# Shorter float16 routing chain, expert indices asked for earlier, and eight expert blocks loaded ahead in a two-block transformer kernel

## The chip, the cores and the metric

The kernel runs on one core of a Trainium2 chip. The metric is the device time of one execution in microseconds (us). Every stage named below runs on the same five engines, each of which works through its own queue of instructions in order: TensorE (PE, matmuls), VectorE (DVE), ScalarE (ACT), GpSimd (POOL) and SyncE (SP, which only issues transfers). A transfer (DMA) is issued from the queue of SP, ACT or POOL, and an instruction that has to wait for a semaphore holds back everything behind it in its queue.

## What is computed

The reference is two transformer blocks of width 1024 on 256 tokens. The change lies in the second half of the first block, a product-key mixture of experts ("peer") with 16384 experts of rank one:

```python
def peer(h, w_pq, sub_keys, u_emb, v_emb):
    q = (h @ w_pq).reshape(B, S, PEER_HEADS, 2, PEER_DHALF)          # 8 heads, two halves of 128
    sc = jnp.einsum("bshcd,hcnd->bshcn", q, sub_keys)                # 128 keys for each half
    s_top, i_top = lax.top_k(sc, PEER_TOPK)                          # best 16 of each half
    cand = s_top[..., 0, :, None] + s_top[..., 1, None, :]
    cand_idx = i_top[..., 0, :, None] * N_KEYS + i_top[..., 1, None, :]
    best, pos = lax.top_k(cand.reshape(B, S, 8, 256), PEER_TOPK)     # best 16 of 256 sums
    expert_idx = jnp.take_along_axis(cand_idx, pos, axis=-1)
    gate = jax.nn.softmax(best, axis=-1)
    ...
    a = gelu(einsum("ced,cd->ce", u_emb[idx], hx)); out = einsum("ce,ced->cd", g * a, v_emb[idx])
```

So every token gets 8 x 16 experts with a gate each. Before it stand the convolution and attention of the first block, behind it the second block; neither is edited.

## The kernel before

**Query stage** (about 276 to 336 us of the profiled execution). The weights of the queries come in 16 chunks of 128x1024, weight numbers 66 to 81. A chunk is loaded by SP, copied rounded by ACT into `whi` (L143), and the remainder `wlo` is `raw - whi`, computed by POOL for the numbers in the table `POOL` and by DVE otherwise (L145, L147). PE then runs 24 matmuls for the chunk (L166 to L168 in turn: each group of three needs `whi` twice and `wlo` once, so a chunk can't get far without its `wlo`), ACT evicts the query as `pq` (L948), and PE and ACT make the scores `sc` (L933, L935) two chunks later.

**Routing chain** on DVE. `unit(tt, h, ..)` finds the top 16 of the two score rows of head h for the token half tt: per row two MAX8, two FIND_INDEX8 and a MATCH_REPLACE8 (`top16`, L850 to L858), then a CAST of the 16 indices into `tops` (L873), then sums of candidates `cd` (L880) and their own top 16 (`best`, `pos`). There are 16 units, 8 for each half. Units, selects and gates stand in a background list `self.bg`, from which `pump` issues a budget of work per chunk (QP) or expert block (UP). `select(tt, h0)` turns four heads' positions into key numbers by a one-hot compare (`eq`, L911), a product with `tops` (L915, by DVE for half 1 and by POOL for half 0) and a sum (L917). `gates(tt)` makes the expert number `ei` and the gate `ex`, and asks for later steps by `later(n, ..)`, n expert blocks behind: `ask` (the pick of indices for the gathered rows, two matmuls of `ei` with `spread` per L1622), `exp`, `softmax` and `turn` (the transposes L986 on PE, and the pick of the gates).

**Which tokens go which way.** Tokens 0 to 159 (N = 160) run dense over all 128 blocks of 128 experts. The other 96 tokens are served by gathered rows: `RowGroup` (`ROWS`: 64 tokens from 192, 32 tokens from 160) fetches, by POOL's indirect DMA (L1632), 128 single expert rows at a time into one of RB = 8 `row` buffers, and DVE takes the dot product (L1637) and later the weighted sum (L1647). `some_rows(RU)` asks for RU of such transfers per u block and `some_rows(RV)` for RV per v block.

**The u stage** (336 to 669 us): per expert block i one load of 512 KB from a ring of ten buffers that are called raw, whi and wlo in turn, 8 matmuls `mm<-hn,raw` (L1031; 16 records in the trace, since each float32 matmul leaves two), and a Gelu on ACT. From the end of `self.bg` on (block `i0`), the one-hot stage runs beside the remaining blocks: 40 groups of four tokens, each with DVE's one-hots `QO` (L1055), ACT's `P`, POOL's `R`, eight matmuls (`place`, L1069) and a multiplication into the matrix G (`put`, L1079).

**The v stage** (674 to 970 us): 4 matmuls with a zero operand open the accumulators (L1146; `zeros` is set by DVE just ahead, L1144), then 123 of the 128 v blocks run with 8 matmuls each (L1141). Every fourth load of v blocks is issued from POOL's queue, the others from SP's, and the gathers run beside it. Between the first 64 blocks and the others `park` (the residual stream) is loaded back as `xo` by POOL's queue (L1158), into space that was that of `G1`.

All from the u stage to the end of the v loop is issued in the order of the program text on every engine (`in_order`).

Of the kernel before, what the change touches and what calls it, by code (L numbers as in the profile page):

```python
# [9 lines left out]
F32 = mybir.dt.float32  # L10
F32R = mybir.dt.float32r
# [12 lines left out]
D = 1024  # L24
# [22 lines left out]

N_WT = 279
# [13 lines left out]
POOL = (*range(4, 52), *range(66, 82))  # L62
# [12 lines left out]
UP = (2.1, 1.4)  # L75

RU = 0.8
RV = 0.8

GL = (2, 3, 4)  # L80
# [3 lines left out]


ROWS = ((192, 64), (160, 32))
# [5 lines left out]
class Kernel:  # L92
# [736 lines left out]
    def peer(self):  # L829
# [11 lines left out]
        gTl = p2h.tile([128, T], F16, name="gTl")  # L841
        sk = p2q.tile([128, 16, 128], F32, name="sk")
# [4 lines left out]
        BIG = -3.0e38  # L847

# [13 lines left out]
        tops = p2t.tile([128, 2, 2, 8, 16], F32, name="tops")  # L862

        def unit(tt, h, scs):
# [3 lines left out]
            for c in range(2):  # L868
# [4 lines left out]
                nc.vector.tensor_copy(tops[:, tt, c, h], iu)  # L873
# [12 lines left out]
        def select(tt, h0, eng):  # L886
# [5 lines left out]
            f = p2t.tile([128, 4, m], F32, name="f", bufs=1)  # L892
# [5 lines left out]
            z = p2t.tile([128, m], F32, name="z", bufs=1)  # L898
# [9 lines left out]
            yield 1.2  # L908
            for c, dst in ((0, isel), (1, jsel)):
                eq = p2t.tile([128, m, 16], F32, name="eq", bufs=1)  # L910
                nc.vector.tensor_tensor(eq, f[:, c, :, None].to_broadcast([128, m, 16]),  # L911
                                  self.iota[:, None, :16].to_broadcast([128, m, 16]), op=ALU.is_equal)
                yield 1.1
                e4 = eq.rearrange("p (h s) a -> p h s a", s=16)
                eng.tensor_tensor(e4, e4, tops[:, tt, c, h0:h0 + nh, None, :].to_broadcast([128, nh, 16, 16]), op=ALU.mult)  # L915
                yield 1.1
                nc.vector.reduce_sum(dst[:, tt, h0:h0 + nh].rearrange("p h s -> p (h s)"), eq, axis=AX.X)  # L917
                yield 1.1
# [41 lines left out]
        def gates(tt):  # L960
# [30 lines left out]
            if tt == 1:  # L991
                self.later(GL[0], ask)
# [8 lines left out]
        pr = self.open("rows", side="right")  # L1001
# [25 lines left out]
        def ublock(i, n_t):  # L1027
            raw = whole(a["ut"][i], i)
# [58 lines left out]
        self.bg[k:k] = [select(1, 0, nc.vector), select(1, 4, nc.vector), gates(1)]  # L1087
        self.bg += [select(0, 0, nc.gpsimd), select(0, 4, nc.gpsimd), gates(0)]
# [46 lines left out]
        zero = self.cp.tile([128, 128], F32R, name="zero")  # L1135
        nc.vector.memset(zero.bitcast(F32), 0.0)
# [574 lines left out]
def _constants():  # L1711
# [3 lines left out]
    def put(name, v):  # L1715
        c[:v.shape[0], CST[name]:CST[name] + v.shape[1]] = v
# [134 lines left out]
```

## Time and profile before

| What | us |
|---|---|
| Median of three runs | 1626.1 |
| The three runs | 1626.78, 1626.1, 1613.58 |
| The profiled execution, its own time | 1624.07 |
| Span of that execution in the trace | 1622.2 |
| PE busy | 1533.6 |
| DVE busy | 1167.7 |
| ACT busy | 645.1 |
| POOL busy | 514.1 |

The rows of the trace have a start (us from the start of the span), a duration, the engine, the line of the program and the operands as out<-in; in brackets stands how long the engine stood idle before, and what ended that. Numbers of buffers are left out. A line of a helper collects all its callers, so a stage is best read by a window of time. Durations of neighbouring matmuls overlap: what a run of them costs is the difference of two starts.

### The profile page before, as it was taken

The numbers are of one execution on the slowest core, as the hardware profiler recorded it, in microseconds if no ns is written. First come the engines' busy times: TensorE is split into PE (matmuls) and PEld (weight loads), VectorE is DVE, ScalarE is ACT, GpSimd is POOL, SyncE is SP. The second block draws the span as 40 slices with busy tenths as digits, with TensorE's granted clock in tenths as the row PEclk, the third lists the DMA queues.
The fourth block names the chain that finished last, engine by engine and source line by source line (L and its number), as shares of the span: only waits on it lengthen the run. The fifth ranks groups of instructions, "written<-read, shape, count | busy, mean of one in ns | idle before, by whom it ended". The sixth has DMA issues, their size and how long they took to land.

```text
span 1622.2 us, 29850 instructions
## 1 busy us (share of the span) xinstructions
PE 1533.6 (95%) x11502; PEld 1469.1 (91%) x11502; DVE 1167.7 (72%) x2549; ACT 645.1 (40%) x1387; POOL 514.1 (32%) x379
## 2 busy tenths in 40 slices
PE   8989989996989999999979999999999999999997
PEld 7877989996989999899979999898999998899986
DVE  6998888998888889744434447977777557776755
ACT  4566655531155444100000005366555455654543
POOL 3734632701576777655444520100000020000000
PEclk9999999997999999999989999999999999999999
DMA  5523446475999999999999984743765677366653
GB/s 187 169 91 98 131 139 222 141 248 221 332 349 404 397 393 394 347 409 409 409 374 409 409 344 153 251 126 109 225 185 187 188 191 220 117 195 183 182 185 114
DMA packets 109389, 398.97 MB, mean 246 GB/s; under 512 B 12484, under 2 KB 12643, under 8 KB 108736
## 3 DMA queue, kind: packets, MB, share of 16 engines
q1 hardware_dynamic: 73872, 266.37, 48.3%
q0 software_dynamic: 35232, 130.64, 21.4%
q8 instruction: 90, 1.47, 0.4%
q14 instruction: 51, 0.42, 0.1%
q10 hardware_dynamic: 144, 0.07, 0.0%
HBM read 394.86 MB, written 6.11 MB: 247 GB/s over the span
## 4 chain that ended last, share of the span: by engine, by line
PE 69%; DVE 17%; DMA 7%; issue 3%; ACT 2%; POOL 2%; SPq 0%; POOLq 0%; DVEq 0%; ACTq 0%
PE ax L1141 12%; PE mm L1031 12%; PE mm L166 11%; PE mm L167 11%; PE mm L168 11%; DMA raw<-vv 5%; DVE ax L617 2%; PE mm L234 2%; PE mm L232 2%; PE mm L233 1%; DVE wlo L147 1%; PE ax L1069 1%; DVE junk L1637 1%; DMA raw<-wst 1%; PE ax L471 1%
## 5 line engine op out<-in xcount | busy, mean ns | idle before, releaser
L143 ACT ACTIVATE whi<-raw 128x1024 fp32r<-128x1024 f32 x275 | 290.0, 1058 | 609.3 <-DMA raw<-wst 304.0
L147 DVE TENSOR_TENSOR wlo<-raw,whi 128x1024 fp32r<-128x1024 f32 x211 | 258.0, 1225 | 116.5 <-ACT whi L143 112.5
L166 PE MATMUL mm<-xgh,whi 128*128 128x256 f32 x1064 | 304.1, 286 | 0.0
L167 PE MATMUL mm<-xgl,whi 128*128 128x256 f32 x1064 | 301.1, 283 | 2.6 <-DVE xgl L406 2.6
L168 PE MATMUL mm<-xgh,wlo 128*128 128x256 f32 x1064 | 300.7, 283 | 0.4 <-DVE wlo L147 0.4
L1647 DVE SCALAR_TENSOR_TENSOR acc<-row,w,acc 128x1024 f32<-128x1024 f32 x94 | 120.8, 1285 | 155.1 <-DMA row<-vv,idx 154.8
L167 PEld LDWEIGHTS mm<-xgl,whi 128*128 128x128 f32 x1064 | 201.8, 190 | 3.0 <-DVE xgl L406 2.8
L166 PEld LDWEIGHTS mm<-xgh,whi 128*128 128x128 f32 x1064 | 201.6, 190 | 2.0 <-issue 1.3
L168 PEld LDWEIGHTS mm<-xgh,wlo 128*128 128x128 f32 x1064 | 201.8, 190 | 0.7 <-DVE wlo L147 0.6
L145 POOL TENSOR_TENSOR wlo<-raw,whi 128x1024 fp32r<-128x1024 f32 x64 | 153.8, 2411 | 129.4 <-ACT whi L143 127.7
L1632 POOL DMA_INDIRECT row<-vv,idx x96 | 124.0, 1292 | 89.5 <-DMA row<-vv,idx 61.3
L1632 POOL DMA_INDIRECT row<-un,idx x96 | 110.2, 1147 | 110.4 <-DVE idf L1626 54.3
L1141 PE MATMUL ax<-G,raw 128*128 128x160 f32 x832 | 124.2, 303 | 10.8 <-DMA raw<-vv 10.8
L1141 PEld LDWEIGHTS ax<-G,raw 128*128 128x128 f32 x832 | 117.1, 192 | 12.0 <-DMA raw<-vv 12.0
L1031 PE MATMUL mm<-hn,raw 128*128 128x160 f32 x816 | 121.1, 303 | 1.8 <-issue 1.8
L1637 DVE CUSTOM_DVE_ANT_0 junk<-row,h 128x1024 f32<-128x1024 f32 x96 | 120.5, 1255 | 0.5
L1031 PEld LDWEIGHTS mm<-hn,raw 128*128 128x128 f32 x816 | 114.5, 192 | 2.4 <-issue 2.4
L167 PE MATMUL mm<-hl,whi 128*128 128x256 f32 x368 | 106.6, 290 | 2.2 <-DVE hl L377 2.1
L1141 PE MATMUL ax<-G,wlo 128*128 128x160 f32 x608 | 94.1, 308 | 9.8 <-DMA wlo<-vv 9.6
L1141 PEld LDWEIGHTS ax<-G,wlo 128*128 128x128 f32 x608 | 88.2, 196 | 11.4 <-DMA wlo<-vv 11.3
L617 DVE SCALAR_TENSOR_TENSOR ax<-u,cw,ax 128x256 f32<-128x256 f32 x227 | 97.4, 482 | 0.6
L1031 PE MATMUL mm<-hn,wlo 128*128 128x160 f32 x608 | 93.3, 308 | 0.0
(437 smaller groups left out, 3361.7 us busy)
## 6 DMA issues: line engine op xcount, KB each, us to landing
raw<-wst SPq DMA_DIRECT2D x278, 512.0 KB
raw<-ut SPq DMA_DIRECT2D x51, 512.0 KB
raw<-vv SPq DMA_DIRECT2D x40, 512.0 KB
whi<-ut SPq DMA_DIRECT2D x39, 512.0 KB
wlo<-ut SPq DMA_DIRECT2D x38, 512.0 KB
whi<-vv SPq DMA_DIRECT2D x32, 512.0 KB
wlo<-vv SPq DMA_DIRECT2D x25, 512.0 KB
wlo<-vv POOLq DMA_DIRECT2D x13, 512.0 KB
```

The lines of the kernel that those rows point to most:

```text
L143: nc.scalar.activation(hi, raw, AF.Copy)
L145: nc.gpsimd.tensor_sub(lo, raw, hi)
L147: self.pin = nc.vector.tensor_sub(lo, raw, hi)
L166: nc.tensor.matmul(pt, w[:, s], xs[0][:, k], start=first, stop=False)
L167: nc.tensor.matmul(pt, w[:, s], xs[1][:, k], start=False, stop=False)
L168: nc.tensor.matmul(pt, lo[:, s], xs[0][:, k], start=False, stop=last)
L617: nc.vector.scalar_tensor_tensor(y[:, c] if k == 30 else ps, u[:, c, k:k + T], cw[:, c, k:k + 1], ps, op0=ALU.mult, op1=ALU.add)
L1031: nc.tensor.matmul(pt, raw[:, k * 128:(k + 1) * 128], hn[:, k, :N], start=(k == 0), stop=(k == C - 1))
L1141: nc.tensor.matmul(acc[d // 2][:, d % 2, :N], raw[:, d * 128:(d + 1) * 128], G(i), start=False, stop=False, skip_group_check=True)
L1632: self.k.nc.gpsimd.indirect_dma_start(t, None, table, bass.IndirectOffsetOnAxis(ap=self.idx[:, s:s + 1], axis=0))
L1637: self.k.nc.vector.tensor_tensor_reduce(junk, row, self.h, 1.0, 0.0, ALU.mult, ALU.add, self.a[:, s:s + 1])
L1647: self.k.nc.vector.scalar_tensor_tensor(self.acc, row, w, self.acc, op0=ALU.mult, op1=ALU.add)
```

## The change

1. `tops` becomes float16 and holds each index 16 times over. It is written by POOL (32 CASTs of 128x256, `tops<-iu`) instead of DVE (32 CASTs of 128x16).
2. `select` works in float16: `eq` is laid out so that the last dimension is contiguous in every operand, both halves' products run on DVE, and the sum is four float16 additions (8, 4, 2 and 1 of 16) instead of a reduction.
3. Weight numbers 70 and 76 leave the table `POOL`, so DVE makes their `wlo`.
4. The `rows` pool is opened before the query stage, and its eight buffers receive the first eight u blocks, issued from ACT's queue. The ring starts with block 8, and the v blocks' numbering with 120 instead of 128.
5. The tables `spread`, `fold` and `own` of each row group are loaded from the constants (two transfers on ACT's queue), where six DVE operations had made them.
6. `ask` comes 1 block behind gates(1) (was 2, with `exp`); `exp`, `softmax` and `turn` come 4, 6 and 8 blocks behind (were 2, 3, 4). UP, RU and RV are 1.5/1.3, 0.85 and 0.78 (were 2.1/1.4, 0.8 and 0.8), and some costs of background steps are other numbers.
7. The zero operand of the accumulators' opening is a 128x128 tile that POOL sets early; 16 matmuls of 128 columns replace the 4 of 512. The 512 column `zeros` tile is gone. `pg` and `rows` are closed in the other order, and `xo` then lies elsewhere: the load of `xo` waits for `R` (POOL) and `P` (ACT) of the one-hot stage, and no longer for the last matmul of the first 64 v blocks.

```diff
-POOL = (*range(4, 52), *range(66, 82))
+POOL = (*range(4, 52), *range(66, 70), *range(71, 76), *range(77, 82))
...
-UP = (2.1, 1.4)
-RU = 0.8
-RV = 0.8
-GL = (2, 3, 4)
+UP = (1.5, 1.3)
+RU = 0.85
+RV = 0.78
+AL = 1
+GL = (4, 6, 8)
...
+        zero = self.cp.tile([128, 128], F32R, name="zero")
+        nc.gpsimd.memset(zero.bitcast(F32), 0.0)
...
+        pr = self.open("rows", side="right")
+        first = [pr.tile([128, D], F32, name="row", bufs=RB) for _ in range(RB)]
+        for i, raw in enumerate(first):
+            nc.scalar.dma_start(raw, a["ut"][i])
...
-        tops = p2t.tile([128, 2, 2, 8, 16], F32, name="tops")
+        tops = p2t.tile([128, 2, 2, 8, 16, 16], F16, name="tops")
+        num = p2t.tile([128, 16, 16], F16, name="num")
+        nc.gpsimd.tensor_copy(num, self.iota[:, :16, None].to_broadcast([128, 16, 16]))
...
-                nc.vector.tensor_copy(tops[:, tt, c, h], iu)
+                nc.gpsimd.tensor_copy(tops[:, tt, c, h], iu[:, :, None].to_broadcast([128, 16, 16]))
...
-                eq = p2t.tile([128, m, 16], F32, name="eq", bufs=1)
-                nc.vector.tensor_tensor(eq, f[:, c, :, None].to_broadcast([128, m, 16]),
-                                  self.iota[:, None, :16].to_broadcast([128, m, 16]), op=ALU.is_equal)
-                e4 = eq.rearrange("p (h s) a -> p h s a", s=16)
-                eng.tensor_tensor(e4, e4, tops[:, tt, c, h0:h0 + nh, None, :].to_broadcast([128, nh, 16, 16]), op=ALU.mult)
-                nc.vector.reduce_sum(dst[:, tt, h0:h0 + nh].rearrange("p h s -> p (h s)"), eq, axis=AX.X)
+                eq = p2t.tile([128, nh, 16, 16], F16, name="eq", bufs=1)
+                nc.vector.tensor_tensor(eq, f[:, c].rearrange("p (h s) -> p h s", s=16)[:, :, None].to_broadcast([128, nh, 16, 16]),
+                                        num[:, None].to_broadcast([128, nh, 16, 16]), op=ALU.is_equal)
+                nc.vector.tensor_mul(eq, eq, tops[:, tt, c, h0:h0 + nh])
+                for n in (8, 4, 2):
+                    nc.vector.tensor_add(eq[:, :, :n], eq[:, :, :n], eq[:, :, n:2 * n])
+                nc.vector.tensor_add(dst[:, tt, h0:h0 + nh], eq[:, :, 0], eq[:, :, 1])
...
             if tt == 1:
-                self.later(GL[0], ask)
+                self.later(AL, ask)
...
-            raw = whole(a["ut"][i], i)
+            raw = first[i] if i < RB else whole(a["ut"][i], i - RB)
...
-        zeros = pgb.tile([128, 512], F32R, name="zeros")
-        nc.vector.memset(zeros.bitcast(F32), 0.0)
         for q in range(4):
-            nc.tensor.matmul(acc[q].rearrange("p a b -> p (a b)"), zero, zeros, start=True, stop=False, skip_group_check=True)
-        nv = 128
+            for k in range(4):
+                nc.tensor.matmul(acc[q].rearrange("p a b -> p (a b)")[:, k * 128:(k + 1) * 128], zero, zero, start=True, stop=False, skip_group_check=True)
+        nv = 128 - RB
...
+        self.close("pg")
         self.close("rows")
-        self.close("pg")
```

ACT's queue at the start of the query stage, before. The rows 268, 270 and 273 are `whi` of weights 69, 70 and 71; the `pq` are the evicted query chunks 66, 67 and 68.

```order
267 L323 ACTIVATE sqq<-x 128x256
268 L143 ACTIVATE whi<-raw 128x1024
269 L948 ACTIVATE pq<-mm 128x256
270 L143 ACTIVATE whi<-raw 128x1024
271 L372 ACTIVATE rb<-ax 128x256
272 L948 ACTIVATE pq<-mm 128x256
273 L143 ACTIVATE whi<-raw 128x1024
274 L935 ACTIVATE sc<-ax,rr 128x128 x2
275 L948 ACTIVATE pq<-mm 128x256
```

The same place of ACT's queue after the change (`row<-ut` are the loads of the first eight u blocks):

```order
267 L328 ACTIVATE sqq<-x 128x256
268 L859 DMA row<-ut 128x1024 x8
269 L964 ACTIVATE pq<-mm 128x256
270 L377 ACTIVATE rb<-ax 128x256
271 L964 ACTIVATE pq<-mm 128x256 x2
272 L148 ACTIVATE whi<-raw 128x1024
273 L951 ACTIVATE sc<-ax,rr 128x128 x4
274 L148 ACTIVATE whi<-raw 128x1024
275 L951 ACTIVATE sc<-ax,rr 128x128
276 L148 ACTIVATE whi<-raw 128x1024
```

The eight loads stand ahead, and the next `whi` (row 272, that of weight 69) has moved behind three `pq`, the last of which needs query chunk 68 to be finished on PE.

POOL's queue from the query stage to the first gathers (`row<-un`), before: 16 `wlo` with nothing among them but the load of `park`.

```order
14 L145 TENSOR_TENSOR wlo<-raw,whi 128x1024 x48
15 L843 DMA sk<-subk 128x2048
16 L145 TENSOR_TENSOR wlo<-raw,whi 128x1024 x2
17 L834 DMA park<-x 128x2048
18 L145 TENSOR_TENSOR wlo<-raw,whi 128x1024 x14
19 L1632 DMA row<-un,idx_4203 128x1024 x10
20 L915 TENSOR_TENSOR eq<-eq,tops 128x1024
```

The last part of the same stretch after the change; the six `wlo` shown are those of weights 75, 77, 78, 79, 80 and 81.

```order
26 L150 TENSOR_TENSOR wlo<-raw,whi 128x1024
27 L888 CAST tops<-iu 128x256 x3
28 L150 TENSOR_TENSOR wlo<-raw,whi 128x1024
29 L888 CAST tops<-iu 128x256
30 L150 TENSOR_TENSOR wlo<-raw,whi 128x1024
31 L888 CAST tops<-iu 128x256 x2
32 L150 TENSOR_TENSOR wlo<-raw,whi 128x1024
33 L888 CAST tops<-iu 128x256 x2
34 L150 TENSOR_TENSOR wlo<-raw,whi 128x1024
35 L888 CAST tops<-iu 128x256 x2
36 L150 TENSOR_TENSOR wlo<-raw,whi 128x1024
37 L888 CAST tops<-iu 128x256 x9
```

Casts 1 to 15 of `tops`, each of which needs a FIND_INDEX8 of DVE, now stand ahead of the `wlo` of weight 81 in the same queue (13 of them ahead of that of weight 80).

## Rows read from the trace of the kernel before

**Rows 1.** The page: the transfer rate in 40 slices of the span.
```profile
GB/s 187 169 91 98 131 139 222 141 248 221 332 349 404 397 393 394 347 409 409 409 374 409 409 344 153 251 126 109 225 185 187 188 191 220 117 195 183 182 185 114
```
**Rows 2.** Page, the chain that ended last: shares of the span by engine.
```profile
PE 69%; DVE 17%; DMA 7%; issue 3%; ACT 2%; POOL 2%; SPq 0%; POOLq 0%; DVEq 0%; ACTq 0%
```
**Rows 3.** Waits of PE, 336 to 976 us: total us, times, longest.
```profile
PE ax L1622 <- DVE ei L964: 13.0, 1, 13.0
PE ax L1141 <- DMA raw<-vv: 10.8, 5, 2.8
PE ax L1141 <- DMA wlo<-vv: 9.6, 2, 9.3
PE ax L986 <- DVE ex L978: 4.5, 1, 4.5
PE ax L1146 <- DVE zeros L1144: 3.4, 1, 3.4
PE ax L986 <- DVE jsel L917: 2.8, 1, 2.8
```
**Rows 4.** Windows: length, busy by engine (instructions), PE clock, DMA share, GB/s.
```profile
455.00:669.50 214.50, 214.35 (x1746) 212.59 (x1745) 180.92 (x372) 101.86 (x384) 149.75 (x113) 1.00 1.00 386
...
676.00:800.00 124.00, 117.14 (x849) 115.81 (x849) 60.04 (x57) 0.23 (x1) 69.09 (x62) 1.00 1.02 402
800.00:850.00 50.00, 40.74 (x283) 40.50 (x281) 19.27 (x15) 0.00 (x0) 20.15 (x21) 0.90 0.97 381
```
**Rows 5.** Timeline of PE, 331 to 367 us: the first u block.
```profile
335.88 1.80 PE L1031 MATMUL mm<-hn,raw 128*128 128x160 f32 x12
```
**Rows 6.** Timeline of PE, 377 to 395 us: the pick of the indices.
```profile
378.81 1.19 PE L1622 MATMUL ax<-ei,spread 128*128 128x128 f32 x4 [12.97 <-DVE ei L964]
379.79 4.16 PE L1031 MATMUL mm<-hn,wlo 128*128 128x160 f32 x16
383.79 2.34 PE L1031 MATMUL mm<-hn,raw 128*128 128x160 f32 x16
385.96 0.61 PE L1622 MATMUL ax<-ex,spread 128*128 128x128 f32 x4
```
**Rows 7.** Timeline of PE, 446 to 468 us: behind gates(0).
```profile
451.02 4.38 PE L1031 MATMUL mm<-hn,wlo 128*128 128x160 f32 x16
...
459.58 0.22 PE L1069 MATMUL ax<-P,QO 128*128 128x128 f16 x1
```
**Rows 8.** Timeline of PE, 818 to 838 us: the longest wait of the v stage.
```profile
832.57 4.63 PE L1141 MATMUL ax<-G,wlo 128*128 128x160 f32 x16 [9.26 <-DMA wlo<-vv]
```
**Rows 9.** Timeline of POOL, 800 to 835 us: its queue in that wait.
```profile
823.94 0.57 POOL L1158 DMA_DIRECT2D xo<-park  x1 [19.45 <-PE ax L1141]
824.50 0.57 POOL L1019 DMA_DIRECT2D wlo<-vv  x1
```
**Rows 10.** Timeline of DVE, 296 to 302 and 349 to 359 us: casts, one unit.
```profile
300.69 1.35 DVE L873 CAST tops<-iu 128x16 f32<-128x16 uint32 x1
...
351.49 0.17 DVE L873 CAST tops<-iu 128x16 f32<-128x16 uint32 x1
...
353.45 0.28 DVE L850 MAX8 tv<-sc 128x8 f32<-128x128 f32 x1
...
358.88 0.18 DVE L893 TENSOR_SCALAR q<-pos 128x64 uint32<-128x64 uint32 x1
```
**Rows 11.** Timeline of POOL, 282 to 342 us: two of the query stage's remainders.
```profile
299.61 2.41 POOL L145 TENSOR_TENSOR wlo<-raw,whi 128x1024 fp32r<-128x1024 f32 x1 [0.81 <-ACT whi L143]
302.88 2.40 POOL L145 TENSOR_TENSOR wlo<-raw,whi 128x1024 fp32r<-128x1024 f32 x1 [0.87 <-ACT whi L143]
```
**Rows 12.** Groups of DVE by form, 336 to 560 us: count, busy us, mean ns.
```profile
L1055 DVE TENSOR_TENSOR QO<-io,jiT 128x512 f16<-128x512 f16 x44 | 18.2, 459 | 11.3 <-PE ax L1069 10.4 <-issue 0.8
L911 DVE TENSOR_TENSOR eq<-f,iota 128x1024 f32<-128x1024 f32 x8 | 9.8, 1223 | 0.1
...
L902 DVE TENSOR_TENSOR f<-f,z 128x64 f32<-128x64 f32 x4 | 0.9, 225 | 0.1
```

More of the change, by code (lines that the diff above doesn't have):

```diff
@@ L46 @@
 N_CST = _n
+ROWS = ((192, 64), (160, 32))
+for _t0, _w in ROWS:
+    CST[f"rows{_t0}"] = N_CST
+    N_CST += 128 + _w + 128 // _w
 N_WT = 279
@@ L884, in unit, with select @@
             yield from top16(best[:, tt, h], pos[:, tt, h], cd, w)
-        def select(tt, h0, eng):
+        def select(tt, h0):
             nh = 4
@@ L897, in select @@
             nc.vector.tensor_copy(f, q)
-            z = p2t.tile([128, m], F32, name="z", bufs=1)
+            z = p2t.tile([128, m], F16, name="z", bufs=1)
             nc.vector.tensor_scalar(z, f[:, 0], 4.0, None, op0=ALU.is_ge)
@@ L1000, in peer @@
         Gs = [pg.tile([128, 64, N], F32, name="G0")]
-        pr = self.open("rows", side="right")
         rows = [RowGroup(self, pr, hn, ei, ex, *g) for g in ROWS]
@@ L1086, in peer @@
         k = next((k for k, u in enumerate(self.bg) if k and u not in firsts), len(self.bg))
-        self.bg[k:k] = [select(1, 0, nc.vector), select(1, 4, nc.vector), gates(1)]
-        self.bg += [select(0, 0, nc.gpsimd), select(0, 4, nc.gpsimd), gates(0)]
+        self.bg[k:k] = [select(1, 0), select(1, 4), gates(1)]
+        self.bg += [select(0, 0), select(0, 4), gates(0)]
         order = self.in_order()
@@ L1172, in peer @@
         pw = self.open("pw", side="right")
-        ends = [(i, whole(a["vv"][i], nv + i)) for i in range(64 - LAST, 64)]
+        ends = [(i, whole(a["vv"][i], nv + i - 64 + LAST)) for i in range(64 - LAST, 64)]
         g12 = self.small.tile([128, 8], F32, name="g12", bufs=1)
@@ L1596, in __init__ @@
         self.w = pool.tile([128, n], F32, name=f"w{t0}")
-        self.fold = pool.tile([128, n], F32, name=f"fold{t0}")
-        nc.vector.reduce_sum(self.fold, k.ident.rearrange("p (c t) -> p t c", t=n), axis=AX.X)
-        self.own = pool.tile([128, self.copies], F32, name=f"own{t0}")
-        nc.vector.reduce_sum(self.own, k.ident.rearrange("p (c t) -> p c t", t=n), axis=AX.X)
-        self.spread = pool.tile([128, 128], F32, name=f"spread{t0}")
-        o = t0 % 128
-        nc.vector.tensor_copy(self.spread.rearrange("p (c t) -> p c t", t=n), k.ident[:, None, o:o + n].to_broadcast([128, self.copies, n]))
+        c = pool.tile([128, 128 + n + self.copies], F32, name=f"c{t0}")
+        o = CST[f"rows{t0}"]
+        nc.scalar.dma_start(c, k.a["cst"][:, o:o + 128 + n + self.copies])
+        self.spread, self.fold, self.own = c[:, :128], c[:, 128:128 + n], c[:, 128 + n:]
     def activations(self):
@@ L1750, in _constants @@
     put("onehot", oh)
+    p = np.arange(128)
+    for t0, w in ROWS:
+        put(f"rows{t0}", np.concatenate([p[:, None] == t0 % 128 + p[None] % w, p[:, None] % w == np.arange(w)[None],
+                                         p[:, None] // w == np.arange(128 // w)[None]], 1).astype(f))
     return c
```

12 lines of the change are left out of this document (4 added, 8 removed).

## The prediction

> **What bounds the kernel now.** I read the chain that ended last first: 69% of it lies on PE and 17% on DVE [rows 2], so a microsecond counts where PE stands still or runs at its lower clock. Then PE's waits over the stage that the diff touches: six of them make 44 us, each with one named cause [rows 3]. Then the timelines of PE around the long ones, to see what follows a wait, and the queue of the engine that was waited for. The pick of the indices stands 12.97 us for DVE's `ei`, and the block behind it takes 4.0 us (379.79 to 383.79) where the next takes 2.17 (383.79 to 385.96) [rows 6]: after a long stand PE runs at half clock for a while. The same follows gates(0), where PE waits 2.8 and 4.5 us and a block then lasts 4.38 instead of 2.34 [rows 3, 6, 7]. In the v stage one wait of 9.26 us, followed by a block of 4.63, is for a load in POOL's queue [rows 8]; POOL had itself stood 19.45 us in front of the load of `xo`, and the awaited load is the very next instruction [rows 9]. Elsewhere in the u stage PE is full (214.35 of 214.5 us) [rows 4].
>
> The v stage has a second limit. A v block moves 1.8 x 524288 bytes (its own load and 0.8 gathers). In the 2.17 us that its matmuls need this would be 435 GB/s, but the best slices show 409 [rows 1], so a block costs 2.31 us there by transfers, and PE stands 10.8 us in small waits for `raw` [rows 3].
>
> **Query stage: a cost.** In PE's groups of three matmuls every third needs `wlo`. POOL made 16 of them, one per 3.27 us (299.61 to 302.88), each 2.41 us long [rows 11]; PE had no wait of that kind, and its first u block starts at 335.88 [rows 5]. Now 15 casts stand ahead of the `wlo` of weight 81 in POOL's queue, and each waits for DVE. A unit of DVE takes 353.45 to 358.88 = 5.43 us [rows 10] and brings two casts. The first cast came at 300.69 [rows 10]; I put it at 299.3, since casts and weights 70 and 76 leave the contest with POOL described below. The fifteenth belongs to the eighth unit: 299.3 + 7 x 5.43 = 337.3. No cast of 128x256 on POOL is in the trace. Its bounds are 0.17 us, DVE's small cast, and a quarter of the 2.41 us that POOL takes for 128x1024, 0.6 [rows 10, 11]; I take 0.3. Then `wlo` 81 runs from 337.6 to 340.0, the last chunk takes 3.27, and a little low clock and the last scores about 1: the u stage starts at 344.3, **8.4 us later**. If units are faster or the first cast earlier it is 4; if casts take 0.6 and DVE waits, 14. The loads of the eight first blocks, on ACT's queue, cost 8 issues of at most 0.57 us (POOL's issue, [rows 9]), 4.6 us, and push `whi` of weight 69 behind chunk 68. PE then stops early for about 4 us, but this is not added: the last `wlo` decides when the stage ends. `wlo` 70 and 76 cost DVE 1.22 us each, by the nearest two-input operation [rows 12]; that is inside the 5.43 per unit, which had casts that go.
>
> DVE's cast at 300.69 took 1.35 us and ended with POOL's `wlo` of 299.61 + 2.41 = 302.02; alone it takes 0.17 [rows 10, 11]. So DVE stands while POOL works on SBUF, and taking casts from DVE removes such stops. If a cast on POOL holds DVE in the same way, the two `cd` sums right behind it wait up to 0.6 us in each of seven units, and the stage costs 4 us more. The Trainium skill, "SBUF — State Buffer", section "Who interferes with whom", states this as a rule: POOL and a DVE instruction with two SBUF inputs lock each other out for a whole instruction, whoever comes first. By that rule, the trace agrees for the long `wlo` against DVE's cast; no row shows a short POOL cast against DVE.
>
> **The pick: a gain.** Before, PE reached it at 378.81 - 12.97 = 365.84, after 12 blocks [rows 6]. Now 14 blocks stand ahead: 344.3 + (365.84 - 335.88) + 2 x 2.17 = 378.6. DVE is there earlier. Selecting took 358.88 to about 378.7 [rows 6, 10]. Per half and key, three operations of 1.22 us [rows 12] become two float16 operations on 1024 elements and four sums. The float16 `QO` on 512 elements takes 0.459 where 64 float32 elements take 0.225 [rows 12]; scaled, a 1024 element operation is 0.7 to 0.8, and the sums 0.2 to 0.45 each. That is 2.65 instead of 3.67, four times: 4 us less. With the casts and the six table operations gone, `ei` is ready near 371.5; without any float16 gain near 376, still ahead of PE. So the stand of 12.97 and the 1.8 of low clock behind it go. PE leaves the pick (0.98 us [rows 6]) with 14 blocks done at 379.6, and had 14 done at 385.96: **6.4 us ahead**, the query stage's 8.4 included. What comes next is the gathers on POOL, with eight late casts among them; each waits half a unit, 2.7 us, which is about the pace at which 0.85 gathers per block are wanted (2.17 / 0.85 = 2.6), so I add nothing.
>
> **gates(0): a gain.** The two waits (7.3 us) and the slow block (2.0) go: **9.3 us**. DVE's way to it is shorter by the float16 select, by the casts, and by products that it no longer awaits from POOL; `turn` stands 8 blocks behind instead of 4, and the first placement on PE comes after 48 blocks instead of 41 (counted in the order). PE comes only 6.4 us earlier, so a cover of four blocks, 8.7 us, hides what is left.
>
> **One-hot stage: a small cost.** The same 40 groups now share 80 blocks, not 87. The stage shrinks from 214.5 to 199.3 us, and DVE's 180.92 us [rows 4] become 91% of it instead of 84%; RU of 0.85 raises the demand on transfers from 386 [rows 4] to about 392 GB/s, under 409. Neither is over its limit, but slack for in-order waits is smaller: I take **2 us**, with bounds of 0 and 10 (the stage at its old length but for 5 us).
>
> **Opening of the accumulators: a gain.** PE waits 3.4 us for DVE to set `zeros` [rows 3]. That work is gone, but the accumulators still wait for the last products out of the same PSUM banks. Between 0 and 3.4 I take **2.5**.
>
> **The v stage: a gain.** `xo` waits no longer for PE, so POOL's queue moves on: 9.26 us and the 2.3 of low clock behind them [rows 8], 11.6. Against that stands the transfer limit. In the window of the stall the rate fell only from 402 to 381 GB/s [rows 4], which is 2.6 us of transfers; with RV 0.78 a block needs 2.28 instead of 2.31, 3.1 us over 123 blocks. If transfers alone set the stage it gains 5.7; if PE does, 11.6 + 3.1 = 14.7. I take **10**.
>
> **Sum.** -6.4 - 9.3 + 2 - 2.5 - 10 = -26.2 us. From the profiled execution's 1624.07 this gives **1598**. That execution lies 2 us under the median of 1626.1, and one of the three runs was 12.5 below the median. Around 16 us (1%) is what a measurement of this kernel can tell from no change.
>
> **Rivals.**
> - *Transfers take the gain back.* The v stage gains 5.7 and the tighter one-hot stage loses 10: 1598 + 4.3 + 8 = **1610**. For it: five slices at 409 GB/s look like a ceiling [rows 1], and small `raw` waits are spread over the v stage [rows 3]. Against it: in 676 to 800 the rate is 402, and PE busy 117 of 124 [rows 4].
> - *The query stage costs almost nothing and PE sets the v stage.* With the casts 4 us earlier and 14.7 in the v stage: **1589**. For it: DVE units were held by POOL before; against it: the fifteenth cast can't come ahead of seven units.
> - *POOL's casts hold DVE*, 4 us more as worked out above: **1602**. For it: the cast of 1.35 us; against it: the sums are short and may come before POOL begins.
> - *POOL's queue makes it slower.* If every one of the 11 `wlo` behind a cast came late, not the last alone, each chunk would wait 2.41 and run 3.27 us slow at half clock, less some overlap, about 5.1: 56 us instead of 8.4, which gives **1646**. From 3.1 us per chunk (34.6 in all) the change gains nothing; from 4.6 it is slower by 1%. For it: strict order in POOL's queue and the low clock after each stand [rows 6]. Against it: DVE needs 5.43 us for two casts and PE 6.54 for two chunks, so DVE catches up.
> - *Nothing moves much*: `ei` late all the same and the v stage bound by transfers: 1598 + 12 + 6, **1616**.
>
> **Chances.** Forecast 0.38, POOL's casts hold DVE 0.12, cheap query stage 0.13, transfers 0.17, nothing much 0.10, POOL's queue 0.10. The likeliest alone spans 1588 to 1606. To leave out no more than 2 in 10 the range goes from 1583 to 1615. Faster by over 1% (under 1610) is the first three and half of the transfers: 0.63 + 0.09 = 0.72; slower is the queue: 0.10; the rest 0.18.
>
> **What would show it.** In the profile after: the first u block near 344, with waits of PE for `wlo` of POOL at the last chunks; no wait for `ei` or `ex` and a pick near 379; the accumulators opened near 655; no POOL stand ahead of `xo` and v blocks at 2.28 to 2.31 us. The prediction is wrong if the first u block comes past 355, if PE waits for DVE in the one-hot stage, or if the waits for `raw` grow by more than what the `xo` stall gave.

## The result and the profile after

The changed kernel takes 1597.5 us (median of four runs, 1592.9 to 1600.1) where the kernel before took 1625.4 in the same comparison: a ratio of 0.983, 95% interval 0.980 to 0.985. The prediction was 1598. The span fell from 1622.2 to 1595.0 us.

The page of the changed kernel: transfer rate in 40 slices of about 40 us, then the chain that ended last by engine.

```profile
GB/s 190 164 101 94 124 130 212 255 157 209 409 409 409 409 409 409 391 408 409 409 409 409 409 232 187 245 120 130 223 185 185 184 193 205 134 192 183 177 190 111
...
PE 65%; DMA 17%; DVE 11%; issue 4%; ACT 2%; POOL 1%; SPq 0%; POOLq 0%; DVEq 0%; ACTq 0%
```

Against [rows 1, 2] the rate now stands at 409 GB/s from the eleventh slice to the twenty-third with hardly a dent, and transfers have gone from 7% to 17% of the chain. The longest of PE's waits from 276 to 960 us (line waited for, total us, times, longest), to set beside [rows 3]:

```profile
PE ax L1154 <- DMA raw<-vv: 9.0, 3, 8.3
PE mm L173 <- POOL wlo L150: 7.6, 5, 2.0
PE ax L1154 <- DMA whi<-vv: 5.1, 3, 3.8
PE ax L1154 <- DMA wlo<-vv: 3.1, 2, 2.7
```

All waits for `ei`, `ex`, `jsel` and `zeros` are gone. New are 7.6 us for POOL's `wlo` in the query stage, and one wait of 8.3 us for the load of the first v block. PE's timeline at the steps of the prediction (start, length, operands, idle before), first of the changed kernel, then the last three steps of the kernel before:

```profile
345.05 3.70 PE L1046 MATMUL mm<-hn,row 128*128 128x160 f32 x26
...
379.38 0.61 PE L1630 MATMUL ax<-ei,c 128*128 128x128 f32 x4
...
649.11 2.20 PE L1158 MATMUL ax<-zero 128*128 128x128 f32 x16
659.57 4.12 PE L1154 MATMUL ax<-G,raw 128*128 128x160 f32 x16 [8.26 <-DMA raw<-vv]
...
941.51 0.43 PE L1154 MATMUL ax<-G,raw 128*128 128x160 f32 x2
```
```profile
672.76 1.36 PE L1146 MATMUL ax<-zeros,zero 128*128 128x512 f32 x4 [3.40 <-DVE zeros L1144]
674.26 3.79 PE L1141 MATMUL ax<-G,wlo 128*128 128x160 f32 x16
...
970.23 0.43 PE L1141 MATMUL ax<-G,whi 128*128 128x160 f32 x2
```

| Place on PE | before | after | moved by | forecast |
|---|---|---|---|---|
| first u block | 335.88 | 345.05 | +9.2 | +8.4 |
| pick of the indices | 378.81 | 379.38 | | 378.6 |
| end of the u stage | 669.36 | 649.11 | -20.2 | -13.7 |
| first v block | 674.26 | 659.57 | -14.7 | -16.2 |
| v loop ends | 970.23 | 941.51 | -28.7 | -26.2 |

(669.36 is 672.76 less the wait of 3.40. The v loop ends where the last five blocks begin, at 970.23 before and at 941.51 after.)

POOL's queue at the last chunks, at the first gather and at the load of `xo`:

```profile
338.13 0.40 POOL L888 CAST tops<-iu 128x256 f16<-128x256 uint32 x1 [1.11 <-DVE iu L870]
338.49 2.35 POOL L150 TENSOR_TENSOR wlo<-raw,whi 128x1024 fp32r<-128x1024 f32 x1
...
382.43 0.40 POOL L888 CAST tops<-iu 128x256 f16<-128x256 uint32 x1 [26.38 <-DVE iu L870]
384.00 0.44 POOL L888 CAST tops<-iu 128x256 f16<-128x256 uint32 x1 [1.17 <-DVE iu L870]
384.61 1.03 POOL L1640 DMA_INDIRECT row<-un,idx  x1 [0.17 <-issue]
...
785.03 0.57 POOL L1170 DMA_DIRECT2D xo<-park  x1 [0.91 <-DMA row<-vv,idx]
```

The `wlo` of weight 81 begins right behind the fifteenth cast, at 338.49 (forecast 337.6). A cast takes 0.40 us. The first gather waits behind two casts of half 0 and comes 5.2 us behind the pick, where it had come 3.65 behind. POOL stands 0.91 us ahead of `xo`, where it had stood 19.45 [rows 9]. DVE's timeline:

```profile
360.12 0.69 DVE L929 TENSOR_TENSOR eq<-eq,tops 128x1024 f16<-128x1024 f16 x1
...
372.52 0.29 DVE L980 SCALAR_TENSOR_TENSOR ei<-isel,jsel 128x128 f32<-128x128 f32 x1
...
379.80 0.29 DVE L1632 TENSOR_TENSOR own<-ax,c 128x128 f32<-128x128 f32 x1 [6.18 <-PE ax L1630]
```

The float16 select runs at the forecast price (0.69 against 1.22 us [rows 12]) and `ei` is there at 372.5, 7 us ahead of PE. The last row is what I had not thought of: DVE's queue stands 6.18 us in front of the first operation behind the pick, so half 0's units, and with them the casts that POOL holds ahead of the gathers, wait too. Windows of the changed kernel (length; busy of PE, PE's weight loads, DVE, ACT, POOL, with counts; PE clock; DMA share; GB/s):

```profile
400.00:649.00 249.00, 249.00 (x2005) 247.48 (x2004) 228.88 (x508) 106.93 (x397) 176.84 (x136) 1.00 1.03 409
649.00:660.00 11.00, 2.74 (x21) 2.48 (x20) 9.67 (x18) 0.59 (x3) 6.59 (x6) 0.67 0.98 369
660.00:920.00 260.00, 251.08 (x1810) 248.98 (x1810) 114.58 (x91) 0.00 (x0) 133.10 (x121) 0.99 1.03 408
920.00:942.00 22.00, 22.00 (x164) 22.00 (x163) 9.06 (x8) 1.06 (x1) 0.97 (x1) 1.00 0.89 342
```

PE has no idle time and full clock for 249 us, with DVE at 92%, and transfers at 409 GB/s. Then PE stands for one load. Whether it has outrun the loads as a whole is taken up below.

### The profile page after: what moved, and what is told of

The parts are those of the page before. It is cut to its first block, busy times and chain, and to the rows that moved or that the text cites. A ratio compares the mean times of both kernels' runs of the same rounds, so it can differ in the third digit from the quotient of the medians.

```text
span 1595.0 us, 29881 instructions
## 1 busy us (share of the span) xinstructions
PE 1525.9 (96%) x11514; PEld 1462.2 (92%) x11514; DVE 1150.4 (72%) x2535; ACT 641.4 (40%) x1378; POOL 512.7 (32%) x407
## 3 DMA queue, kind: packets, MB, share of 16 engines
HBM read 395.04 MB, written 6.11 MB: 252 GB/s over the span
## 4 chain that ended last, share of the span: by engine, by line
PE 65%; DMA 17%; DVE 11%; issue 4%; ACT 2%; POOL 1%; SPq 0%; POOLq 0%; DVEq 0%; ACTq 0%
PE mm L1046 17%; DMA row<-vv,idx 14%; PE mm L171 11%; PE mm L173 11%; PE mm L172 11%; PE ax L1154 2%; DVE ax L622 2%; PE mm L239 2%; PE mm L237 2%; PE mm L238 2%; DVE wlo L152 1%; PE ax L1084 1%; DMA wlo<-vv 1%; POOL wlo L150 1%; DMA raw<-vv 1%
## 5 line engine op out<-in xcount | busy, mean ns | idle before, releaser
L148 ACT ACTIVATE whi<-raw 128x1024 fp32r<-128x1024 f32 x275 | 290.1, 1058 | 591.8 <-PE ax L1154 281.9
L150 POOL TENSOR_TENSOR wlo<-raw,whi 128x1024 fp32r<-128x1024 f32 x62 | 148.7, 2406 | 127.5 <-ACT whi L148 125.8
L1046 PE MATMUL mm<-hn,raw 128*128 128x160 f32 x768 | 112.6, 300 | 0.0
L1046 PEld LDWEIGHTS mm<-hn,raw 128*128 128x128 f32 x768 | 106.3, 190 | 0.0
L1154 PE MATMUL ax<-G,whi 128*128 128x160 f32 x624 | 95.4, 303 | 5.1 <-DMA whi<-vv 5.1
L1154 PEld LDWEIGHTS ax<-G,whi 128*128 128x128 f32 x624 | 89.1, 193 | 6.0 <-DMA whi<-vv 5.9
L1154 PE MATMUL ax<-G,wlo 128*128 128x160 f32 x608 | 90.2, 300 | 3.1 <-DMA wlo<-vv 3.1
```

What stands on the lines that cost most here:

```text
L148: nc.scalar.activation(hi, raw, AF.Copy)
L150: nc.gpsimd.tensor_sub(lo, raw, hi)
L1046: nc.tensor.matmul(pt, raw[:, k * 128:(k + 1) * 128], hn[:, k, :N], start=(k == 0), stop=(k == C - 1))
L1154: nc.tensor.matmul(acc[d // 2][:, d % 2, :N], raw[:, d * 128:(d + 1) * 128], G(i), start=False, stop=False, skip_group_check=True)
```

## The experiments

Two theories stood against each other. *Stands add up*: each stand of PE costs what it lasts, as in the sum. *Transfers limit*: from the first gathers on, 409 GB/s set the time, and what PE gains is given back in waits for loads. The query stage does not begin at the same time in every execution (the matmul that waits for `xgl` begins between 279.3 and 282.9), so the stages are compared from that matmul, called the mark below. The first three columns of numbers are us from the mark, the last is a length; each row is one execution:

| Kernel | first u block | first gather | u stage ends | from there to the end of the v loop |
|---|---|---|---|---|
| before | 53.4 | 100.0 | 386.9 | 300.9 |
| after | 63.0 | 102.6 | 367.1 | 292.4 |
| after, second time | 64.8 | 104.3 | 368.9 | 292.4 |
| xo waits again | 64.7 | 104.3 | 368.8 | 298.4 |
| half of the gathers | 61.6 | 101.2 | 365.7 | 269.4 |
| pick after 11 blocks | 62.9 | 96.2 | 367.1 | 291.2 |
| casts on DVE | 57.9 | 94.7 | 362.2 | 293.0 |
| casts late | 55.4 | 91.9 | 359.5 | 294.5 |
| casts late, second time | 55.4 | 91.9 | 359.5 | 294.8 |
| casts late, pick after 12, RV 0.76 | 55.9 | 90.1 | 361.3 | 289.1 |
| first blocks by the ring | 64.6 | 100.2 | 364.7 | 292.8 |
| lags 2, 3, 4 | 63.0 | 102.5 | 368.8 | 292.8 |
| before, part 7 alone | 53.5 | 100.0 | 383.9 | 297.0 |

### Half of the gathers

```diff
-            begun.append((g, f, s, g.row(tables[f], s)))
+            begun.append((g, f, s, begun[-1][3] if s % 2 else g.row(tables[f], s)))
```

> The changed kernel with every second gathered row left out: DVE's dot products and sums take the neighbour's row again, so all of DVE's, PE's and ACT's work stays and half of the gathers' bytes go (a part of the computation is wrong by that). If transfers set the v stage, the stand of 8.3 us at its first block, the small waits (8.9 us) and the low clock behind them (about 4) go, and the v loop runs at PE's 2.17 us per block, 268 instead of 281.9 us: 1597.5 - 8.3 - 1.8 - 14 = 1573. If the waits come from the issue of the loads (queues, buffers) and not from the amount of bytes, they stay: 1595 to 1598.

One execution took 1572.8 us. This kernel leaves out every second gathered row. PE's timeline:

```profile
648.60 2.20 PE L1158 MATMUL ax<-zero 128*128 128x128 f32 x16
650.63 2.39 PE L1154 MATMUL ax<-G,raw 128*128 128x160 f32 x16
...
918.00 0.43 PE L1154 MATMUL ax<-G,raw 128*128 128x160 f32 x2
```

The u stage is the same, the wait at its end and all waits in the v loop are gone, and 123 blocks take 267.4 us, 2.17 each. With the same instructions on PE and DVE and half of the gathers, 23 us go (292.4 to 269.4). That the gathers cost this time is shown. Whether they do it by their bytes or by their place in POOL's queue, this run does not separate, since half of POOL's gathers went with the bytes.

The traces say which loads PE waits for. Every fourth v block is loaded from POOL's queue, block 0 among them. In the changed kernel SP had issued the loads of blocks 1 to 3 by 634.83 us, and POOL issued that of block 0 at 645.81, behind its gathers:

```profile
629.97 0.33 SPq L1034 DMA_DIRECT2D whi<-vv  x1
632.66 0.33 SPq L1034 DMA_DIRECT2D wlo<-vv  x1
634.83 0.33 SPq L1034 DMA_DIRECT2D raw<-vv  x1
```
```profile
645.81 0.60 POOL L1034 DMA_DIRECT2D raw<-vv  x1
```

All eight waits of PE over 0.15 us in this v loop are for loads that POOL issued (blocks 0, 44, 60, 64, 84, 88, 100 and 112), and so are all seven in the kernel before. Behind the wait of 8.26 us PE runs on to block 44 without another one. In the second execution of the changed kernel, where PE begins block 0 at 657.1, blocks 1 and 2 had landed at 640.6 and 643.2. So the ring of buffers was not empty: one load was late, and those behind it lay ready. Time from issue to landing of the v loads issued between 662 and 918 us, in the second execution of the changed kernel (POOL's, then SP's) and with half of the gathers (the same):

```profile
DMA to landing us min/median/max: 12.9/16.8/20.2
DMA to landing us min/median/max: 6.7/7.6/9.5
```
```profile
DMA to landing us min/median/max: 4.5/5.4/7.9
DMA to landing us min/median/max: 4.2/7.0/10.0
```

With all gathers beside them POOL's loads take twice as long as SP's, with half of them they do not. The rate bears on the sum: 123 blocks of 1.78 x 512 KB (the load and 0.78 gathers) at 409 GB/s are 280.7 us (an estimate), and the v loop took 281.9. Had the stretch from 649 to 942 us run at 409 throughout, it would be about 5 us shorter (an estimate from the windows above). No run issues these loads from SP alone, so how much of the stand is the queue's and how much the rate's stays open.

### xo waits for PE again

```diff
+        pad = pgb.tile([128, 256], F32, name="pad")
+        nc.gpsimd.memset(pad[:, :1], 0.0)
         Gs.append(pgb.tile([128, 64, N], F32, name="G1"))
```

> The changed kernel with 1 KB of padding in the pool of G1, so that the load of xo again waits for the last matmul of the first 64 v blocks; all else as changed. If the wait of PE behind POOL's queue is a cost of its own, it comes back whole: 9.3 us of standing and 2.3 of low clock, 1597.5 + 11.6 = 1609. If transfers at 409 GB/s set the time from the first gather to the end of the v loop, PE's stand of about 9 us comes back near 790 to 810 us, but the other waits of the v stage (17.2 us now) shrink by most of it, and only the transfers lost in the stall count (2.6 us in the kernel before): 1597.5 + 2.6 to 5 = 1600 to 1603.

It took 1601.6 us, 0.988 of the kernel before (0.986 to 0.990), against 0.983 for the changed kernel. The kernel before took 1621.0 beside it, so on the scale of the expectation, which counts from 1597.5, this is 1606. PE's and POOL's timelines:

```profile
811.08 4.63 PE L1156 MATMUL ax<-G,whi 128*128 128x160 f32 x16 [9.58 <-DMA whi<-vv]
```
```profile
802.14 0.56 POOL L1172 DMA_DIRECT2D xo<-park  x1 [19.41 <-PE ax L1156]
802.69 0.57 POOL L1034 DMA_DIRECT2D whi<-vv  x1
```

The stand comes back as [rows 8, 9] had it, 9.6 us and a block at half clock; the stretch from the u stage to the end of the v loop grows by 6.0 us (298.4 against 292.4). So neither theory had the size: a stand of 11.9 us with its low clock cost half of itself, and PE waits less for other loads in the same loop behind its first block (4.0 us in all, against 8.9).

### Part 7 alone, in the kernel before

```diff
-            nc.tensor.matmul(acc[q].rearrange("p a b -> p (a b)"), zero, zeros, start=True, stop=False, skip_group_check=True)
+            for k in range(4):
+                nc.tensor.matmul(acc[q].rearrange("p a b -> p (a b)")[:, k * 128:(k + 1) * 128], zero, zero, start=True, stop=False, skip_group_check=True)
```

(with the `zero` tile set early by POOL, and no `zeros`).

> The kernel before with part 7 alone: a 128x128 zero operand that POOL sets early, 16 matmuls, no 512 column tile, and xo clear of G1. If each stand counts whole, 11.6 us for xo and 2.5 to 3.4 for the opening: 14 to 15 us less than the kernel before, a ratio of 0.991. If transfers limit the v stage (the stand cost 6.6 us of v loop in the run that put it back), 6.6 + 2.5 to 3.4: 9 to 10 us, a ratio of 0.994.

It took 1616.6 us, 0.998 of the kernel before (0.996 to 0.999): 3.6 us. On PE:

```profile
666.23 2.20 PE L1145 MATMUL ax<-zero 128*128 128x128 f32 x16
671.10 4.63 PE L1141 MATMUL ax<-G,wlo 128*128 128x160 f32 x16 [2.67 <-DMA wlo<-vv]
```

The wait for `zeros` is gone whole, but the first v block then waits 2.67 us for its load and runs at half clock, and the long stand behind `xo` is gone, while the waits for `raw` rise from 10.8 to 11.8 us. Of the 14 us that I had put on these two stands 3.8 are left between the end of the u stage and the end of the v loop (300.9 to 297.0). The forecast's prices for them were far too high taken alone.

### An earlier pick

```diff
-UP = (1.5, 1.3)
+UP = (2.0, 1.3)
```

> UP = (2.0, 1.3) instead of (1.5, 1.3): the pick of the indices comes after 11 u blocks instead of 14, at 345.05 + 3.7 + 11 x 2.172 = 372.7 instead of 379.4; DVE has ei at 372.8, so PE should stand under 1 us. If transfers set the time from the first gather on, all of the 6.5 us come through: 1591. If PE is the bound and only its own stands count, nothing moves, since PE does not stand at the pick now: 1597 to 1599.

It took 1596.1 us, 0.985 of the kernel before (0.983 to 0.987): no gain. The pick came at 373.33 and the first gather 6.4 us earlier from the mark, the u stage ended at the same place, and the stretch behind it shrank by 1.2 us. So the first gather alone does not set the time either. The gathers are asked for at a pace per block; begun earlier they are over earlier, and in the last 22 us the rate is 293 GB/s, where it was 342 in the changed kernel:

```profile
920.00:942.00 22.00, 21.94 (x162) 21.70 (x161) 6.36 (x5) 1.06 (x1) 0.00 (x0) 1.00 0.78 293
```

(window of this kernel, columns as above).

### The casts on DVE, and the casts late on POOL

```diff
-                nc.gpsimd.tensor_copy(tops[:, tt, c, h], iu[:, :, None].to_broadcast([128, 16, 16]))
+                nc.vector.tensor_copy(tops[:, tt, c, h], iu[:, :, None].to_broadcast([128, 16, 16]))
```

> The 32 casts of tops go back to DVE (in the new float16 form), all else as changed. POOL's queue then holds only wlo, and the u stage should start at 336 to 338 instead of 345.05. DVE pays 24 casts ahead of ei: at 0.3 us each 7 us, and 10 us more where POOL's wlo holds them. So ei comes at 380 to 390 instead of 372.8, PE reaches the pick at 371 and stands 9 to 19 us. Total by first gather: 0 to 10 us later than now, 1598 to 1608. If casts cost DVE only 0.3 us and nothing else, 1597.

It took 1595.4 us, 0.985 (0.983 to 0.987), as the changed kernel within the intervals. The u stage starts 5.1 us earlier from the mark, the cast on DVE takes 0.27 us alone and up to 1.76 where `wlo` holds it, and PE does not stand at the pick (375.37), since `ei` is there at 375.0 and not at 380 to 390. DVE has taken less harm than expected.

```diff
-            nc.gpsimd.tensor_sub(lo, raw, hi)
+            self.last_lo = nc.gpsimd.tensor_sub(lo, raw, hi)
...
+        held, waiting = [True], []
+        def casts(keep):
+            while not held[0] and len(waiting) > keep:
+                with self.tc.issue_after(self.last_lo.ins):
+                    waiting.pop(0)()
...
-                iu = p2t.tile([128, 16], U32, name="iu", bufs=4)
+                iu = p2t.tile([128, 16], U32, name="iu", bufs=32)
-                nc.gpsimd.tensor_copy(tops[:, tt, c, h], iu[:, :, None].to_broadcast([128, 16, 16]))
+                waiting.append(lambda c=c, iu=iu: nc.gpsimd.tensor_copy(tops[:, tt, c, h], iu[:, :, None].to_broadcast([128, 16, 16])))
+                casts(2)
```

(`held` ends behind the last query chunk, and each `select` empties the list.)

> The changed kernel with POOL's casts of tops issued behind the last wlo of the query stage (and a buffer for each index list), so no wlo stands behind a cast. If the 9.2 us by which the u stage starts later than before (345.05 against 335.88) are all due to casts in POOL's queue, it starts at 336. If the eight first loads on ACT's queue hold weight 69's whi and cost their own 4 to 5 us (as the run with the casts on DVE has it, 340.8), it starts at 340.5 to 341.5, PE's waits for wlo fall from 7.6 to about 1.7 us, and the whole kernel gains at most the 4 us: 1591 to 1597.

One execution took 1588.0 us. POOL's and PE's timelines:

```profile
325.09 2.40 POOL L150 TENSOR_TENSOR wlo<-raw,whi 128x1024 fp32r<-128x1024 f32 x1 [0.88 <-ACT whi L148]
327.44 5.77 POOL L896 CAST tops<-iu 128x256 f16<-128x256 uint32 x16
```
```profile
335.18 3.70 PE L1058 MATMUL mm<-hn,row 128*128 128x160 f32 x26
...
369.51 0.61 PE L1642 MATMUL ax<-ei,c 128*128 128x128 f32 x4
```

From the mark the u stage starts 7.6 us earlier than in the changed kernel, and 2.0 us later than in the one before. So of 9.6 us of delay 7.6 are the casts in POOL's queue and 2.0 are left for the rest. (Executions differ here: the changed kernel's second one starts 64.8 us from the mark and not 63.0, the three with late casts at 55.4 to 55.9.) The expectation of 340.5 was wrong, which from the mark would be 58.4: the stop at weight 69 is still there (0.5 and 1.7 us of waits), and no more than 2.0 us are left for it, not 4 to 5. With the casts on DVE the stage took 2.4 us longer than here, of which PE's wait for DVE's `wlo` is 0.7; the rest was not traced. DVE gains as well: `ei` is begun at 363.5, 6.7 us earlier from the mark than in the changed kernel. Both kernels were timed again, beside each other:

> The kernel with the casts issued behind the last wlo, timed in rounds. Its one look had the u stage at 335.2 and the end of the v loop 7.8 us ahead of the changed kernel, of which 2.4 had been there ahead of the query stage. If the 7.5 us that the query stage gives are kept through stages that transfers limit, 0.978 to 0.979 of the kernel before; if transfers take them back, 0.981 to 0.983.

> The changed kernel itself, beside the others on one chip: 0.983 of the kernel before by the ratio that it had on its own chip (0.980 to 0.985).

The changed kernel took 1595.9, a ratio of 0.983 (0.981 to 0.985); with late casts 1590.2, 0.981 (0.979 to 0.983). The stages say that 7.6 us at the end of the u stage shrink to 5.5 or 5.2 at the end of the v loop (9.4 to 7.1, from the changed kernel's second execution); the ratios, with overlapping intervals, can't show it by themselves.

### Late casts, first loads on POOL's queue

```diff
-            nc.scalar.dma_start(raw, a["ut"][i])
+            nc.gpsimd.dma_start(raw, a["ut"][i])
-UP = (1.5, 1.3)
+UP = (1.3, 1.3)
```

> As late, and the eight first loads are issued from POOL's queue, not ACT's, and UP = (1.3, 1.3), so the pick comes after 15 u blocks. The u stage should start at 336 to 337 as before the change, with no wait for wlo at weight 69; the pick at 336.5 + 3.7 + 15 x 2.172 = 372.8, just where DVE has ei. First gather at 378, 6.6 us earlier than in the changed kernel, and one block more done. If the time is set by transfers from there on, 1586 to 1590 on the scale of 1597; if PE's lead is given back in waits for loads, as the 6 us of the run with an earlier pick were, 1593 to 1596.

The premise did not hold: POOL's loads stand in front of `wlo` (PE waits 2.1 us for POOL's and 3.0 for DVE's `wlo`), the u stage starts at 339.38 and the pick comes at 375.88. It took 1590.2 us, 0.980 (0.975 to 0.984), which can't be told from the late casts alone.

### The first blocks by the ring

```diff
-        for i, raw in enumerate(first):
-            nc.scalar.dma_start(raw, a["ut"][i])
-            raw = first[i] if i < RB else whole(a["ut"][i], i - RB)
+            raw = whole(a["ut"][i], i)
-        nv = 128 - RB
+        nv = 128
```

> The changed kernel with part 4 undone: the first eight u blocks come through the ring again, from SP's queue, and the rows' buffers stay empty until the gathers. If the early loads take work out of the stretch that transfers limit, 8 x 1.28 = 10 us come back: 1607. If not, because the ring of ten is refilled between 345 and 384 us, where the rate is 77 to 239 GB/s, and stands ten blocks ahead of PE at the first gather in either kernel, the time stays at 1593 to 1599 and only weight 69's stop on PE (0.5 and 1.7 us) goes.

One execution took 1595.0 us, where the changed kernel beside it took 1595.9. No gain of the early loads shows: before the first gather the rate is low (113 GB/s from 345 to 379 in the changed kernel), so the loads that they replace have room there. They even cost a little. Without them the stop at weight 69 is gone, PE's waits for POOL's `wlo` are 4.5 us instead of 7.6, and the query stage ends 61.0 us from the mark, where the transposes of `hn` begin, and not at 63.0 (64.8 in the second execution of the changed kernel). The rows' buffers being free, the transposes now run ahead of the u stage and not among its first blocks, which moves them and saves nothing:

```profile
340.76 3.77 PE L1620 MATMUL ax<-ident,row 128*128 128x128 f32 x32
```

The u stage ends 4.1 us earlier from the mark than in the changed kernel timed beside it (364.7 against 368.9), and the v loop 3.8 us (657.5 against 661.3); against its first execution (367.1 and 659.5) it is 2.3 and 1.9.

### The lags of gates

```diff
-GL = (4, 6, 8)
+GL = (2, 3, 4)
```

> The changed kernel with exp, softmax and turn 2, 3 and 4 blocks behind gates, as before. If DVE's shorter way to gates(0) alone removed PE's waits of 4.5 and 2.8 us, none come back: jsel of half 0 is ready near 435 and PE reaches the turn near 439. If the later turn was what hid it, PE waits 3 to 7 us there. In either case the time should stay within 3 us of the changed kernel, 1594 to 1600, if transfers set the end of the u stage.

One execution took 1599.1 us. One wait of the old kind is back:

```profile
PE ax L1002 <- DVE ex L994: 1.5, 1, 1.5
```

So of the 7.3 us of stands at gates(0), 1.5 went by the later lags, and the other 5.8 go without them, as DVE's shorter way would have it. Both reasons of the prediction hold, the first being the larger.

### Late casts, a pick after 12 blocks and a lower RV

```diff
-UP = (1.5, 1.3)
+UP = (1.8, 1.3)
-RV = 0.78
+RV = 0.76
```

on top of the late casts.

> As late, with UP = (1.8, 1.3), so the pick comes after 12 blocks, at 335.2 + 3.7 + 12 x 2.172 = 365 where ei is there at 363.8, and RV 0.76. The first gather comes at 367, 4.3 us before late. As the run with an earlier pick alone gave back 5 of 6 us because gathers were then over early in the v stage, a lower RV should keep some of it: 123 x 0.02 x 1.28 = 3.1 us of v loop. Together 2 to 4 us under late, 0.976 to 0.978; if the amount of transfers left at the first gather is all that counts, it equals late.

It took 1587.1 us, 0.977 of the kernel before (0.975 to 0.980), where the changed kernel beside it has 0.983 (0.981 to 0.985). The v loop ends 3.8 us earlier from the mark than with late casts alone (second execution). It is faster than the changed kernel; against late casts alone (0.979 to 0.983) the intervals overlap. That the lower RV, which spreads the gathers over the blocks that are left, keeps the gain of the earlier pick is what I had expected and is not shown: the two edits were not separated.

## Why the prediction was right, and where it was not

**Query stage** (+8.4 forecast, +9.2 measured): right in size and cause. The last `wlo` behind the fifteenth cast decides when the stage ends, and with the casts behind it 7.6 us come back. The cast took 0.40 us, within the bounds.

**POOL's casts hold DVE**: not seen, so the 4 us did not come. What held DVE's `cd` sums was POOL's `wlo`: in the query stage six of the eight sums of 128x48 took 1.3 to 2.1 us, to the end of the `wlo` beside them. A sum that met a cast took 0.2 us like any other (the pair below 0.33), and the cast 0.44 instead of 0.40:

```profile
322.81 2.40 POOL L150 TENSOR_TENSOR wlo<-raw,whi 128x1024 fp32r<-128x1024 f32 x1
350.48 0.44 POOL L888 CAST tops<-iu 128x256 f16<-128x256 uint32 x1 [1.24 <-DVE iu L870]
```
```profile
323.22 2.06 DVE L895 TENSOR_TENSOR cd<-tv 128x48 f32<-128x48 f32 x1
350.33 0.33 DVE L895 TENSOR_TENSOR cd<-tv 128x64 f32<-128x64 f32 x2
```

The Trainium skill, "SBUF — State Buffer", section "Who interferes with whom", has the rule that the prediction cites, of a DVE instruction with two SBUF inputs. By that rule, the trace agrees for these sums, which read two tiles, beside `wlo` (2.06 us instead of 0.20). The cast of 1.35 us, which the prediction set beside the rule, reads one.

**The pick** (378.6 forecast, 379.38 measured): right. That gathers would follow at an unchanged distance was wrong: DVE's stand of 6.18 us at the pick and two casts ahead put the first at 384.6, 2.2 us later than before the change. It cost little: the run with the earlier pick has the first gather 6.4 us earlier and gains 1.2 us by the end of the v loop.

**gates(0)**: right: both waits and the slow block behind them are gone, all 9.3 us.

**One-hot stage**: forecast 2 us of cost, measured none; PE is full to 649 us with DVE at 92%. The transfers stood at 409 GB/s there, not at the forecast 392. The u stage ended 6.5 us earlier than the sum said. 2 us of that are the cost that did not come, and 4.0 are a block that took 6.2 us instead of 2.2 in the profiled execution of the kernel before (first fence) and not in that of part 7 alone (second fence), whose program up to there differs by one small tile:

```profile
391.09 0.30 PE L1031 MATMUL mm<-hn,raw 128*128 128x160 f32 x1
...
397.30 2.34 PE L1031 MATMUL mm<-hn,whi 128*128 128x160 f32 x16
```
```profile
391.05 2.34 PE L1033 MATMUL mm<-hn,raw 128*128 128x160 f32 x16
393.22 2.34 PE L1033 MATMUL mm<-hn,whi 128*128 128x160 f32 x16
```

From the mark the u stage ends at 386.9 in the one and at 383.9 in the other. So about 3 us of the 20.2 that the change seems to gain by the end of the u stage belong to one execution and not to the change. What made that block slow is not known.

**Opening of the accumulators**: the step that failed. I gave it a gain of 2.5 us. The wait for `zeros` did go, but a wait of 8.26 us for the first v block came, with a block at half clock behind it: from the end of the u stage to the first v block 10.5 us instead of 4.9, a loss of 5.6 (8.3 us, and a loss of 3.4, in the second execution). I had priced what PE waited for there and not the load behind it. POOL issues that load, and did so 3.3 us ahead of the end of the u stage (3.6 before the change, at 665.79). PE then began the block 13.8 us after the issue, where with part 7 alone in the old kernel it was 8.2 us (662.94 to 671.10). I had the transfers as a rival for the v loop and the one-hot stage and had not carried it to this place. The run with half of the gathers shows that the gathers are the cause; whether by their bytes or by POOL's queue is open.

**The v stage**: 10 forecast, 14.0 measured from its first block. Opening and v loop belong together: the stand moves between them (8.26 and 281.9 us in the one execution, 6.11 and 284.1 in the other), and their sum was 292.4 in both, against 300.9 before. That is a gain of 8.5 where I had 12.5. Part 7 alone gives 3.8 in the old kernel, and its `xo` half costs 6.0 when undone in the new; the 3.1 us that I gave RV were not tried alone. I had also read the small waits for `raw` [rows 3] as the transfer limit spread over the stage; each of them was for a load in POOL's queue.

So that the total agreed to half a microsecond is luck: the u stage gained 6.5 us more than the sum said, of which about 3 are the execution's own, the stretch behind it gained 4 less, and what lies behind the v loop took 1.5 us longer (653.5 instead of 652.0), for which no cause was looked for. The rival "transfers take the gain back" was at work in the stretch behind the u stage, at a smaller price than I gave it, and not in the one-hot stage.

## What to carry to other kernels

When a change pushes a compute engine ahead, look at each stage's first load: which queue issues it, what stands ahead of it there, and how long such a load takes when the transfer rate is at its highest. The time saved can turn up there as a wait, so price neighbouring stages as one. When a wait names a load, look whether the loads behind it had been issued earlier: then the queue is a suspect beside the rate. A short instruction put in an in-order queue costs what it waits for, not what it lasts (15 casts of 0.40 us ahead of the last `wlo` cost 7.6 us at the start of the u stage, which came back when the casts were issued behind it). Preloading eight blocks brought nothing here, where the loads that it replaced ran at 113 GB/s; in a stretch where transfers are full it was not tried. And profile the kernel before a second time: one slow block of one execution was worth 3 us in the account above.

## What the runs showed of the hardware

The transfer rate of one core held 408 to 409 GB/s for over 500 us (400 to 649 and 660 to 920 us of the changed kernel) with 512 KB loads and gathers of rows mixed. Beside these gathers 512 KB loads from POOL's queue took 16.8 us to land and those from SP's 7.6 (medians of one execution); with half of the gathers it was 5.4 and 7.0. A PE wait of 8.3 us is followed by a block at half clock (4.12 instead of 2.34 us; the granted clock was 0.50 from 654 to 660 us), as before the change. A stand of PE of 11.9 us in the v loop, its low clock included, made the stretch 6.0 us longer. A DVE sum of two inputs took up to 2.06 us instead of 0.20 beside a subtraction of 2.40 us on POOL.
